# Head 0's k and v into early rows, a priority for weight pieces, and 2600 more projection columns ahead of the first scan

## The chip, the cores and the metric

The kernel runs on one core of a Trainium2 chip. TensorE (PE) multiplies, VectorE (DVE) and ScalarE (ACT) work element by element, GpSimd (POOL) does a few of the same, and SyncE (SP) issues nearly all DMA transfers. The metric is the device time of one execution in microseconds (us), as the median over several runs; lower is better.

## The reference

One layer of a hybrid backbone. 512 latent and 256 context tokens of width 2048 are normalised and modulated, and go through one input projection. Group A is a gated delta rule with 8 heads; group B is attention with 8 query and 2 key heads. Both are gated, concatenated and go through one output projection. What matters here is group A:

```python
qkv = jax.nn.silu(centred_conv(qkv, conv_w))          # 5 taps along the tokens
q, k, v = split(qkv)                                  # per head, 128 wide
q = l2_norm(q) * (HEAD_DIM ** -0.5)
k = l2_norm(k)
g = -jnp.exp(a_log) * jax.nn.softplus(gates + dt_bias)
...
g_c = jnp.cumsum(g)                                   # inside a chunk of 64 tokens
t_inv = triangular_solve(eye + a, eye)                # a: 64 x 64, from k, beta and g_c
u = t_inv @ (v_c * b_c)
w = t_inv @ (k_beta * jnp.exp(g_c))
s_final, o = lax.scan(step, s0, (q_c, k_c, u, w, g_c, intra))
```

The scan runs over 12 chunks, once in each direction.

## The kernel before

Matrices are multiplied in full 32-bit precision as three matmuls of a reduced format: each operand is split into a high and a low half (`whi`, `wlo`). A weight piece is 512 rows by 128 columns: SP loads it (`wraw`), ACT casts the high half (L129), DVE subtracts for the low half (L130). Each of the three has three buffers in turn, so piece i can be cast only when PE has left piece i - 3.

**The stages.** Up to about 157 us the modulation is computed while k, v and q of head 0 and k and q of head 1 are projected into five PSUM banks (`klat`, `vlat`, `qlat`, `cctx` for the context part). The first weights are read by ACT and POOL. The second stage, up to about 240 us, prepares head 0 (`gdn_prep(0)`) while PE projects other columns. Then come eight scans (`gdn_scan`), each beside the preparation of the next head, then attention and the output projection.

**Second stage.** `take` (L195) copies a projected bank to SBUF: into one of three rows `craw`, whose memory only becomes free when the first stage's pool `p0` closes, or into one of two rows `xraw`, which have a pool of their own. Then `gdn_post_k`, `_q` and `_v` run the convolution: ACT starts it (`cacc`, one buffer), DVE adds four taps for latent and context tokens (L221), ACT takes a tanh (L224, L225), DVE makes the SiLU (L237) and writes `kq`, `kc` or `vv`. The gates run beside it: `gates(0, 1)` for head 0 and `gates(1, 8)` for the rest give log decays `gg` on DVE, PE sums them along the chunk (`gcp`, `gtot`, L547 to L551), ACT takes exponentials (L553 to L558), and PE transposes the sums (`gtr`).

**`gdn_prep`.** PE transposes k and q (`t1`, `t2`, `t3`, L640 to L653), ACT copies them and takes sums of squares (L643, L649, L657), PE makes the products `gq` (L693) and `gc` (L709). DVE forms the triangular matrix (`gr`) and transposes blocks of it (`NT`, L718). SP sends them through DRAM (`nd`) into another layout (`NE`), DVE inverts 16 x 16 blocks there in 14 steps (L738, L740), and SP brings them back through DRAM (`DD`, L758). DVE transposes (`DT`, L763), and three rounds on PE (`pxa`, `pxb`, `pxy`) join the blocks to the inverse `UU`, which the scan's first matmul reads (`tsh`, L875). `t1`, `t3` and `gc` share one PSUM bank, `t2` and `gq` another.

**What sets the order.** PE's order is as written (`manual_schedule`): a generator `feed` gives the projection matmul by matmul, and `pull(n)` takes n columns of it between two steps of the preparation or the scan. On ACT, DVE, POOL and SP a scheduler orders the instructions when the program is built, by priorities and by times that it estimates; `tc.high_priority(offset=...)` moves what stands under it ahead. On the chip each engine runs its list in order. Tiles of the projection are named by their target: `kvl`, `kvx` are keys and values of the attention (latent, context), `q0a` the queries of its head 0, `vl`, `kl`, `ql` v, k and q of the delta rule.

Of the kernel before, what the change touches and what calls it, by code (L numbers as in the profile page):

```python
# [8 lines left out]
F32 = mybir.dt.float32  # L9
# [59 lines left out]
def build(tc, a):  # L69
    nc = tc.nc  # L70
    V, S, G, T, SY = nc.vector, nc.scalar, nc.gpsimd, nc.tensor, nc.sync
# [31 lines left out]
    def hpass(k, hi, lo):  # L103

        return (hi, [t[:, k] for t in hh]), (hi, [hl(m, k) for m in range(2)]), (lo, [t[:, k] for t in hh])
# [20 lines left out]
    def split(raw, nm, lo_eng=None):  # L126
        hi = wp.tile([128, 512], F32R, tag="whi", bufs=3, name=f"whi_{nm}")
        lo = wp.tile([128, 512], F32R, tag="wlo", bufs=3, name=f"wlo_{nm}")
        S.copy(hi, raw)  # L129
        (lo_eng or G).tensor_tensor(out=lo, in0=raw, in1=hi, op=ALU.subtract)  # L130
        return hi, lo

    def wpiece(src, nm, shape, lo_eng=None):
        raw = wp.tile([128, 512], F32, tag="wraw", bufs=3, name=f"wraw_{nm}")
        v = raw
        if shape is not None:
            v = raw.rearrange("p (a b) -> p a b", b=shape)
        SY.dma_start(v, src)
        hi, lo = split(raw, nm, lo_eng)
        if shape is not None:  # L140
            hi = hi.rearrange("p (a b) -> p a b", b=shape)
            lo = lo.rearrange("p (a b) -> p a b", b=shape)
        return hi, lo

    def mm3(out, lh, ll, rh, rl, start, stop):
        T.matmul(out, lhsT=lh, rhs=rh, start=start, stop=False, skip_group_check=True)  # L146
        T.matmul(out, lhsT=lh, rhs=rl, start=False, stop=False, skip_group_check=True)  # L147
        T.matmul(out, lhsT=ll, rhs=rh, start=False, stop=stop, skip_group_check=True)  # L148

    def proj_tile(col, nm, pl, pc=None):  # L150
        for _ in proj_steps(col, nm, pl, pc):
            pass

    def proj_steps(col, nm, pl, pc=None):


        for kq in range(4):
            src = w_in[kq * 512:(kq + 1) * 512, col:col + 128].rearrange("(k p) c -> p k c", p=128)
            hi, lo = wpiece(src, f"{nm}_{kq}", 128, V)
            passes = [(kq * 4 + k4, n, lw, rt) for k4 in range(4)  # L160
                      for n, (lw, rt) in enumerate(hpass(kq * 4 + k4, hi[:, k4], lo[:, k4]))]

            def one(out, m, k, n, lw, rt):
                T.matmul(out, lhsT=lw, rhs=rt[m], start=k == 0 and n == 0, stop=k == KT - 1 and n == 2,  # L164
                         skip_group_check=True)

            if pc is not None and kq == 0:
                for out, m, n_ in ((pl, 0, SEQ), (pc, 1, CTX)):
                    for x in passes:
                        one(out, m, *x)  # L170
                        yield n_
                continue
            for x in passes:
                one(pl, 0, *x)
                if pc is not None:
                    one(pc, 1, *x)
                yield SEQ if pc is None else SEQ + CTX
# [11 lines left out]
    def btile(shape, nm):  # L189
        return PB.tile(shape, F32, tag="b", name=nm)  # L190

    def stile(shape, nm, tag):
        return PQ.tile(shape, F32, tag=tag, name=nm)

    def take(pl, pc, raw=None, eng=None):  # L195

        raw = next_craw() if raw is None else raw
        copy = S.copy if eng is None else eng.tensor_copy
        if pc is not None:
            copy(raw[:, 2:2 + CTX], pc)  # L200
        copy(raw[:, CTX + 4:CTX + 4 + SEQ], pl)
        return raw

    def conv(t, nm, raw, ctx):

        n = SEQ + (CTX + 2 if ctx else 0)
        off = n - SEQ
        if not ctx:
            raw = raw[:, CTX + 2:]
        acc = cvp.tile([128, 770], F32, tag="cacc", bufs=CA_BUFS, name=f"cacc_{nm}")  # L210
        acc = acc[:, :n]

        def w(j):
            return cvT[:, j * 24 + t:j * 24 + t + 1]

        e = raw[:, 2:]
        S.activation(acc, raw[:, 0:n], AF.Copy, scale=w(0))
        for i0, m in ((off, SEQ), (0, CTX))[:2 if ctx else 1]:
            for j in range(1, 5):
                x = acc[:, i0:i0 + m]  # L220
                V.scalar_tensor_tensor(out=x, in0=raw[:, i0 + j:i0 + j + m], scalar=w(j), in1=x,  # L221
                                       op0=ALU.mult, op1=ALU.add)
        if ctx:
            S.activation(e[:, :CTX], acc[:, :CTX], AF.Tanh)  # L224
        S.activation(e[:, off:off + SEQ], acc[:, off:], AF.Tanh)  # L225
        return acc, e, off
# [27 lines left out]
    es_x = ExitStack()  # L254
    px_ = es_x.enter_context(tc.tile_pool(name="px", bufs=1, side="right", reuse_waits="tile"))
    xraw = [px_.tile([128, 774], F32, name=f"xraw{i}") for i in range(2)]
# [229 lines left out]
    klat = PP.tile([128, SEQ], F32, tag="pl", name="klat0")  # L486
    vlat = PP.tile([128, SEQ], F32, tag="pl", name="vlat0")
    qlat = stile([128, SEQ], "qlat0", "o")
    klat1 = stile([128, SEQ], "klat1", "k")
    qlat1 = stile([128, SEQ], "qlat1", "s")  # L490
    cctx = PC.tile([128, 2, CTX], F32, tag="pc", name="cctx0")
    cctx1 = btile([128, 2, CTX], "cctx1")
# [74 lines left out]

    es_c = ExitStack()
    cvp = es_c.enter_context(tc.tile_pool(name="cvp", bufs=1, reuse_waits="tile"))
    craw = [cvp.tile([128, 774], F32, name=f"craw{i}") for i in range(3)]  # L570
    for t in craw + xraw:
        for i in (0, CTX + 2, NTOK + 4):
            G.memset(t[:, i:i + 2], 0.0)
    ncraw = [0]

    def next_craw():

        ncraw[0] += 1
        return craw[ncraw[0] % 3]

    qkp = es_g.enter_context(tc.tile_pool(name="qkp", bufs=1, reuse_waits="tile"))
    o_d = dram.tile([8, 128, SEQ], F32, name="o_d")
# [5 lines left out]
    def kq_of(h):  # L588
        if h not in kqs:
            kqs[h] = qkp.tile([128, 8, 128], F32, tag="kq", bufs=3, name=f"kq{h}")  # L590
        return kqs[h]
# [12 lines left out]
    def gdn_post_q(h, raw):  # L604
        kq = kq_of(h)
        acc, e, off = conv(h, f"q{h}", raw, False)
        x, y = [t[:, :SEQ].rearrange("p (c t) -> p c t", t=64) for t in (acc, e)]
        silu(V, kq[:, 0:4, 64:128], x[:, 0:4], y[:, 0:4])
        silu(V, kq[:, 4:8, 0:64], x[:, 4:8], y[:, 4:8])

    def gdn_post_v(h, raw):
        vv = vvs[h] = qkp.tile([128, 6, 2, 64], F32, tag="vv", bufs=1, name=f"vv{h}")
        acc, e, off = conv(16 + h, f"v{h}", raw, True)
        for p0_, n, o in ((2, 4, off), (0, 2, 0)):
            x, y = [t[:, o:o + n * 128].rearrange("p (c t) -> p c t", t=64) for t in (acc, e)]
            silu(V, vv[:, p0_:p0_ + n, 0], x[:, 0:n], y[:, 0:n])
            silu(V, vv[:, p0_:p0_ + n, 1], x[:, n:2 * n][:, ::-1], y[:, n:2 * n][:, ::-1])
# [415 lines left out]
        return tc.high_priority(offset=2500)  # L1033

    with tc.high_priority(offset=4000):
        raws = [take(klat, cctx[:, 0]), take(qlat, None), take(vlat, cctx[:, 1], None, V),
                take(klat1, cctx1[:, 0], xraw[0]), take(qlat1, None, xraw[1])]
    gdn_post_k(0, raws[0])
    gdn_post_q(0, raws[1])
    gdn_post_v(0, raws[2])  # L1040
    gp = es_g.enter_context(tc.tile_pool(name="gp", bufs=1, reuse_waits="tile"))
    ktoks = [gp.tile([128, 6, 2, 128], F32, name=f"ktok{i}") for i in range(2)]
    for i in range(2):
# [54 lines left out]
    def feeding():  # L1098

        yield from feed_kva(0)  # L1100
        yield from feed_qa(0)
        yield from feed_kva(1)
        yield from feed_v(1)
        for h in range(2, NH):
            yield from feed_k(h)
            yield from feed_q(h)
            yield from feed_v(h)
            if h in (3, 5):
                yield from feed_qa(1) if h == 3 else feed_kva(2)
        yield from feed_kva(3)  # L1110
        fed.add("kva")
        for h in range(2, NH):
            yield from feed_qa(h)
        for h in range(NZA):
            yield from feed_za(h)

    feed = feeding()
    debt = [0]

    def pull(n):  # L1120
        debt[0] += n
        while debt[0] > 0:
            c = next(feed, None)
            if c is None:
                debt[0] = 0
                return
            debt[0] -= c

    def run(gen, *pulls):

        for n in pulls:
            pull(n)
            if next(gen, gen) is gen:
                return
        for _ in gen:
            pull(2000)
# [19 lines left out]
    with first_of_all():  # L1156
        next(g1)
    gdn_post_q(1, raws[4])
    es_x.close()
    pull(7000)  # L1160
    next(prep, None)
    run(g1, 7000)
# [2 lines left out]
    UUs.append(gp2.tile([128, 12, 128], F32, name="UU1"))  # L1165
    zero(UUs[1].rearrange("p a d -> p (a d)"))
    run(prep, 5000, 24000, 5000, 7000, 6000)
    tail = None
    for h in range(NH):
        while (h + 1 if h + 1 < NH else "kva") not in fed:  # L1170
# [365 lines left out]
    for c in range(4):  # L1536
# [9 lines left out]
        for k in range(KT):  # L1546
            hi = op_.tile([128, 512], F32R, name=f"wlh{k}")
            lo = op_.tile([128, 512], F32R, name=f"wll{k}")
# [5 lines left out]
        for t in range(4):  # L1554
            ts_ = slice(t * 128, t * 128 + 128)
            f = fr[:, t:t + 1]
# [7 lines left out]
            else:  # L1564
                fl = op_.tile([128, 2], F32, name="fl")
                for q in range(2):
# [3 lines left out]
                    for k in range(KT):  # L1570
                        hi, lo = [w[:, hs] for w in wlast[k]]
# [47 lines left out]
```

## Time and profile before

| What | Value |
|---|---|
| Median of 3 runs (lowest to highest) | 1296.88 us (1294.81 to 1297.11) |
| The profiled execution | 1292.93 us, of which its span is 1291.1 us |
| PE busy, share of the span | 1241.8 us, 96% |
| DVE busy | 849.4 us, 66% |
| ACT busy | 580.7 us, 45% |
| Mean granted TensorE clock | 0.991 |
| 160 to 180 us: busy PE, DVE, ACT; clock | 19.74, 15.40, 13.35 us; 0.85 |
| 180 to 200 us: busy PE, DVE, ACT; clock | 17.86, 19.70, 11.51 us; 1.00 |

The trace's times start at the first instruction of the span. A row of the timeline gives start, length, engine, line, operation, the tile that is written and those that are read; in brackets stands how long the engine was idle before it and which instruction released it. Rows of neighbouring instructions overlap a little. A wait for several engines is put down to the one that came last. "issue" is a time in which the engine waited for nothing that the profile shows.

### The profile page before, as it was taken

Reading aid. Unit: us, or ns where it says so; the run is one execution under the profiler, and the core shown is the slowest. Engines: PE = TensorE matmul, PEld = TensorE weight load, DVE = VectorE, ACT = ScalarE, POOL = GpSimd, SP = SyncE. Lnnn points to the kernel's source line nnn. Section 1 sums busy time; section 2 is a strip of 40 time slices with the busy share of each in tenths; the row PEclk is TensorE's granted clock in tenths of the full one; section 3 lists DMA queues with packets and bytes.
Section 4 is the critical chain, followed back from the end, with each engine's and each line's share of the span. In section 5 each row is a group of like instructions: output and inputs, shape, how many; then the busy total and the mean of one; then the engine's idle time right before and its main releaser. Section 6 shows DMA issues by size and latency. Waiting matters only on the chain. (4 is left out here: it accounts for less than half of the span.)

```text
span 1291.1 us, 24373 instructions
## 1 busy us (share of the span) xinstructions
PE 1241.8 (96%) x9242; PEld 1015.1 (79%) x9242; DVE 849.4 (66%) x1905; ACT 580.7 (45%) x1452; POOL 142.7 (11%) x206
## 2 busy tenths in 40 slices
PE   6899999999999999999999999999999999999997
PEld 4566688878788888888888787777888888788886
DVE  5444586686876769676786646546998997555333
ACT  5222363444545454454644444444455544434211
POOL 1323100111111111111211111100000000000000
PEclk9899999999999999999999999999999999999999
DMA  9999424232222312322232445347445353576302
GB/s 355 319 334 346 134 67 106 55 75 56 67 68 75 72 51 71 76 62 65 62 72 63 104 93 150 102 132 255 136 139 156 109 144 97 174 236 195 90 33 98
DMA packets 227288, 164.53 MB, mean 127 GB/s; under 512 B 62242, under 2 KB 198523, under 8 KB 226147
## 3 DMA queue, kind: packets, MB, share of 16 engines
q1 hardware_dynamic: 226874, 162.87, 43.5%
q8 instruction: 73, 1.20, 0.4%
q14 instruction: 44, 0.36, 0.1%
q10 hardware_dynamic: 297, 0.11, 0.0%
HBM read 148.85 MB, written 14.08 MB: 126 GB/s over the span
## 5 line engine op out<-in xcount | busy, mean ns | idle before, releaser
L240 POOL TENSOR_TENSOR sdh<-sth,egl 128x256 f32<-128x256 f32 x80 | 56.8, 711 | 447.9 <-DVE sth L892 345.3
L871 ACT ACTIVATE oqh<-ksh,egsw 64x128 f32<-64x128 f32 x128 | 46.4, 362 | 93.2 <-DVE rh L866 86.9
L866 DVE SCALAR_TENSOR_TENSOR rh<-ksh,negeg,vtokh 64x128 f32<-64x128 f32 x176 | 61.2, 348 | 31.0 <-PE ksh L854 24.4
L146 PE MATMUL po<-whi_wo,mh 128*128 128x512 f32 x192 | 76.2, 397 | 0.0
L148 PE MATMUL po<-whi_wo,ml 128*128 128x512 f32 x192 | 76.0, 396 | 0.0
L147 PE MATMUL po<-wlo_wo,mh 128*128 128x512 f32 x192 | 76.0, 396 | 0.0
L1358 PE MATMUL zl<-hhL,whi_z 128*128 128x512 f32 x176 | 71.4, 405 | 0.0
L1358 PE MATMUL zl<-hL,whi_z 128*128 128x512 f32 x176 | 69.8, 397 | 0.0
L1358 PE MATMUL zl<-hhL,wlo_z 128*128 128x512 f32 x176 | 69.3, 394 | 0.0
L130 DVE TENSOR_TENSOR wlo_wo<-wraw_wo,whi_wo 128x512 fp32r<-128x512 f32 x48 | 33.1, 690 | 51.5 <-ACT whi_wo L129 51.3
L886 PE MATMUL tsh<-vsh,ktok 128*128 128x128 f32 x352 | 56.6, 283 | 6.9 <-ACT vnh L882 3.5
L886 PEld LDWEIGHTS tsh<-vsh,ktok 128*128 128x128 f32 x352 | 47.3, 190 | 16.2 <-ACT vnh L882 8.1
L129 ACT CAST whi_wo<-wraw_wo 128x512 fp32r<-128x512 f32 x48 | 29.7, 620 | 62.3 <-PE po L148 52.1
L892 DVE TENSOR_TENSOR sth<-sdh,tsh 128x256 f32<-128x256 f32 x80 | 33.6, 420 | 27.4 <-PE tsh L886 19.2
L879 ACT ACTIVATE vsh<-tsh,cch 128x128 f32<-128x128 f32 x88 | 32.2, 366 | 38.8 <-PE tsh L875 37.5
L950 ACT CAST pth<-pt 128x512 fp32r<-128x512 f32 x48 | 26.5, 586 | 44.3 <-PE pt L1287 44.3
L164 PE MATMUL vl<-hhL,whi_v 128*128 128x512 f32 x112 | 46.3, 413 | 0.0
L164 PE MATMUL vl<-hhL,wlo_v 128*128 128x512 f32 x112 | 46.2, 413 | 0.0
L164 PE MATMUL vl<-hL,whi_v 128*128 128x512 f32 x112 | 45.8, 409 | 0.0
L1406 DVE SCALAR_TENSOR_TENSOR gacc<-graw,scol,gacc 128x512 f32<-128x512 f32 x60 | 44.9, 748 | 1.1
L146 PEld LDWEIGHTS po<-whi_wo,mh 128*128 128x128 f32 x192 | 36.1, 188 | 9.5 <-ACT ze L1312 0.8
L148 PEld LDWEIGHTS po<-whi_wo,ml 128*128 128x128 f32 x192 | 36.2, 188 | 8.8
(545 smaller groups left out, 3894.5 us busy)
## 6 DMA issues: line engine op xcount, KB each, us to landing
wada<-in_w_ada SPq DMA_DIRECT2D x64, 512.0 KB, 8.4
graw<-in_w_ada SPq DMA_DIRECT2D x64, 256.0 KB, 3.2
wraw_wo<-in_w_out SPq DMA_DIRECT2D x48, 256.0 KB, 3.1
wraw_z<-in_w_in SPq DMA_DIRECT2D x44, 256.0 KB, 3.0
wraw_v<-in_w_in SPq DMA_DIRECT2D x28, 256.0 KB, 2.9
wraw_k<-in_w_in SPq DMA_DIRECT2D x24, 256.0 KB, 2.8
wraw_q<-in_w_in SPq DMA_DIRECT2D x24, 256.0 KB, 2.8
xs<-in_x SPq DMA_DIRECT2D x4, 1024.0 KB, 5.2
```

The lines of the kernel that those rows point to most:

```text
L130: (lo_eng or G).tensor_tensor(out=lo, in0=raw, in1=hi, op=ALU.subtract)
L146: T.matmul(out, lhsT=lh, rhs=rh, start=start, stop=False, skip_group_check=True)
L147: T.matmul(out, lhsT=lh, rhs=rl, start=False, stop=False, skip_group_check=True)
L148: T.matmul(out, lhsT=ll, rhs=rh, start=False, stop=stop, skip_group_check=True)
L164: T.matmul(out, lhsT=lw, rhs=rt[m], start=k == 0 and n == 0, stop=k == KT - 1 and n == 2, skip_group_check=True)
L240: eng.tensor_tensor(out=out, in0=x, in1=y, op=ALU.mult)
L866: V.scalar_tensor_tensor(out=r[rows], in0=ks[rows, d], scalar=gsc["negeg"][rows, gcol:gcol + 1], in1=vtok[rows, p], op0=ALU.mult, op1=ALU.add)
L871: S.activation(oq[rows, v, p - 2], ks[rows, d], AF.Copy, scale=gsc["egsw"][rows, gcol:gcol + 1])
L886: T.matmul(ts[:, d], lhsT=ktok[:, p, half], rhs=vs, start=True, stop=True, skip_group_check=True)
L892: V.tensor_tensor(out=sn, in0=sd, in1=ts[:, 0:2], op=ALU.add)
L1358: T.matmul(pl, lhsT=lw, rhs=rt, start=k == 0 and m == 0, stop=k == KT - 1 and m == 2, skip_group_check=True)
L1406: V.scalar_tensor_tensor(out=acc, in0=raw, scalar=scol[:, k:k + 1], in1=acc, op0=ALU.mult, op1=ALU.add)
```

## The change

Three edits in the second stage. First, head 0's k goes into `xraw[0]` and its v into `xraw[1]`; q of head 0 and k and q of head 1, two of which had those rows, go into `craw`. There are four `craw` rows now, and the pool of `xraw` closes earlier. Second, every weight piece that `proj_steps` loads and splits is given a priority of 2000 (`urgent`) from the start of `feed` until just before the first scan, and 0 after it. Third, `pull(2600)` takes 2600 more columns of projection after the last step of `gdn_prep(0)`, before the scan of head 0.

```diff
--- before.py
+++ after.py
@@ -147,6 +147,8 @@
         T.matmul(out, lhsT=lh, rhs=rl, start=False, stop=False, skip_group_check=True)
         T.matmul(out, lhsT=ll, rhs=rh, start=False, stop=stop, skip_group_check=True)
 
+    urgent = [0]
+
     def proj_tile(col, nm, pl, pc=None):
         for _ in proj_steps(col, nm, pl, pc):
             pass
@@ -156,7 +158,8 @@
 
         for kq in range(4):
             src = w_in[kq * 512:(kq + 1) * 512, col:col + 128].rearrange("(k p) c -> p k c", p=128)
-            hi, lo = wpiece(src, f"{nm}_{kq}", 128, V)
+            with tc.high_priority(offset=urgent[0]):
+                hi, lo = wpiece(src, f"{nm}_{kq}", 128, V)
             passes = [(kq * 4 + k4, n, lw, rt) for k4 in range(4)
                       for n, (lw, rt) in enumerate(hpass(kq * 4 + k4, hi[:, k4], lo[:, k4]))]
 
@@ -567,7 +570,7 @@
 
     es_c = ExitStack()
     cvp = es_c.enter_context(tc.tile_pool(name="cvp", bufs=1, reuse_waits="tile"))
-    craw = [cvp.tile([128, 774], F32, name=f"craw{i}") for i in range(3)]
+    craw = [cvp.tile([128, 774], F32, name=f"craw{i}") for i in range(4)]
     for t in craw + xraw:
         for i in (0, CTX + 2, NTOK + 4):
             G.memset(t[:, i:i + 2], 0.0)
@@ -576,7 +579,7 @@
     def next_craw():
 
         ncraw[0] += 1
-        return craw[ncraw[0] % 3]
+        return craw[ncraw[0] % 4]
 
     qkp = es_g.enter_context(tc.tile_pool(name="qkp", bufs=1, reuse_waits="tile"))
     o_d = dram.tile([8, 128, SEQ], F32, name="o_d")
@@ -1033,11 +1036,12 @@
         return tc.high_priority(offset=2500)
 
     with tc.high_priority(offset=4000):
-        raws = [take(klat, cctx[:, 0]), take(qlat, None), take(vlat, cctx[:, 1], None, V),
-                take(klat1, cctx1[:, 0], xraw[0]), take(qlat1, None, xraw[1])]
+        raws = [take(klat, cctx[:, 0], xraw[0]), take(vlat, cctx[:, 1], xraw[1], V), take(qlat, None),
+                take(klat1, cctx1[:, 0]), take(qlat1, None)]
     gdn_post_k(0, raws[0])
-    gdn_post_q(0, raws[1])
-    gdn_post_v(0, raws[2])
+    gdn_post_q(0, raws[2])
+    gdn_post_v(0, raws[1])
+    es_x.close()
     gp = es_g.enter_context(tc.tile_pool(name="gp", bufs=1, reuse_waits="tile"))
     ktoks = [gp.tile([128, 6, 2, 128], F32, name=f"ktok{i}") for i in range(2)]
     for i in range(2):
@@ -1114,6 +1118,7 @@
         for h in range(NZA):
             yield from feed_za(h)
 
+    urgent[0] = 2000
     feed = feeding()
     debt = [0]
 
@@ -1156,7 +1161,6 @@
     with first_of_all():
         next(g1)
     gdn_post_q(1, raws[4])
-    es_x.close()
     pull(7000)
     next(prep, None)
     run(g1, 7000)
@@ -1165,6 +1169,8 @@
     UUs.append(gp2.tile([128, 12, 128], F32, name="UU1"))
     zero(UUs[1].rearrange("p a d -> p (a d)"))
     run(prep, 5000, 24000, 5000, 7000, 6000)
+    pull(2600)
+    urgent[0] = 0
     tail = None
     for h in range(NH):
         while (h + 1 if h + 1 < NH else "kva") not in fed:
```

PE's order is the same up to the first scan. In three places the order on other engines is this.

ACT at the end of the first projection. `klat_492`, `qlat_494` and `cctx_497` are head 0's, `klat_495`, `qlat_496` and `cctx_498` head 1's; `whi_kv_2` is the third piece of the first attention key projection. Before:

```order
L201 COPY xraw_121<-klat_495 128x512
L200 COPY xraw_121<-cctx_498 128x256
L129 CAST whi_kv_2_1725<-wraw_kv_2_1723 128x512
L201 COPY xraw_122<-qlat_496 128x512
L462 ACTIVATE beta<-gx 128x96
L200 COPY craw_1553<-cctx_497 128x256
L201 COPY craw_1553<-klat_492 128x512
L201 COPY craw_1554<-qlat_494 128x512
L217 ACTIVATE cacc_k_1585<-craw_1553,cvT 128x770
L467 ACTIVATE ug<-ug 128x96
```

With the change:

```order
L204 COPY xraw_121<-klat_492 128x512
L203 COPY xraw_121<-cctx_497 128x256
L129 CAST whi_kv_2_1730<-wraw_kv_2_1728 128x512
L465 ACTIVATE beta<-gx 128x96
L204 COPY craw_1553<-qlat_494 128x512
L203 COPY craw_1554<-cctx_498 128x256
L204 COPY craw_1554<-klat_495 128x512
L204 COPY craw_1555<-qlat_496 128x512
L470 ACTIVATE ug<-ug 128x96
L220 ACTIVATE cacc_k_1589<-xraw_121,cvT 128x770
L129 CAST whi_kv_3_1780<-wraw_kv_3_1778 128x512
```

The copies of `klat_492` and its context now stand ahead of the cast of `whi_kv_2`, the others behind it, and the cast of `whi_kv_3` has moved up behind the start of conv k.

ACT between conv k and the first transposes of head 0. `egl` to `egsw` are the exponentials of the gate sums, `cacc_q` is conv q of head 0. Before:

```order
L129 CAST whi_kv_3_1775<-wraw_kv_3_1773 128x512
L229 ACTIVATE UU_2180<-cmain 128x1536
L217 ACTIVATE cacc_q_1601<-craw_1554,cvT 128x512
L129 CAST whi_q0a_1835<-wraw_q0a_1833 128x512
L558 ACTIVATE egl<-gtot_1744 128x12
L553 ACTIVATE negeg<-gcp_1743 128x12
L554 ACTIVATE esuf<-gcp_1743 128x12
L556 ACTIVATE egsw<-gcp_1743 64x12 x2
L558 ACTIVATE egl<-gcp_1743 128x12
L129 CAST whi_q0a_1879<-wraw_q0a_1877 128x512
L225 ACTIVATE craw_1554<-cacc_q_1601 128x512
```

With the change:

```order
L228 ACTIVATE xraw_121<-cacc_k_1589 128x512
L232 ACTIVATE UU_2184<-cmain 128x1536
L227 ACTIVATE xraw_121<-cacc_k_1589 128x256
L561 ACTIVATE egl<-gtot_1749 128x12
L556 ACTIVATE negeg<-gcp_1748 128x12
L557 ACTIVATE esuf<-gcp_1748 128x12
L559 ACTIVATE egsw<-gcp_1748 64x12 x2
L561 ACTIVATE egl<-gcp_1748 128x12
L220 ACTIVATE cacc_q_1605<-craw_1553,cvT 128x512
L129 CAST whi_q0a_1884<-wraw_q0a_1882 128x512
L228 ACTIVATE craw_1553<-cacc_q_1605 128x512
```

The start of conv q stood ahead of the exponentials and stands behind them now; the casts of `whi_kv_3` and the first `whi_q0a` have left for places further up.

DVE in the preparation of head 0. `grh` is the triangular matrix, `cch` the scale columns, `cacc_k` conv k of head 1, `wlo_kv_0` the low half of the first piece of the second attention key projection. Before:

```order
L240 TENSOR_TENSOR cch_1865<-cch_1865,esuf 128x12
L240 TENSOR_TENSOR IB_1638<-gqh_1886,grh_1785 64x4x64 x4
L221 SCALAR_TENSOR_TENSOR cacc_k_2000<-xraw_121,cvT,cacc_k_2000 128x512
L702 TENSOR_TENSOR grh_1785<-grh_1785,cch_1865 128x768
L221 SCALAR_TENSOR_TENSOR cacc_k_2000<-xraw_121,cvT,cacc_k_2000 128x512
L240 TENSOR_TENSOR grh_1785<-gqh_1886,grh_1785 128x256 x2
L240 TENSOR_TENSOR grh_1785<-gch_1942,grh_1785 128x128 x2
L718 STREAM_TRANSPOSE NTh_1789<-grh_1785 32x6x32 x4
L221 SCALAR_TENSOR_TENSOR cacc_k_2000<-xraw_121,cvT,cacc_k_2000 128x512
L221 SCALAR_TENSOR_TENSOR cacc_k_2000<-xraw_121,cvT,cacc_k_2000 128x256
L130 TENSOR_TENSOR wlo_kv_0_2028<-wraw_kv_0_2025,whi_kv_0_2027 128x512
```

With the change:

```order
L243 TENSOR_TENSOR IB_1643<-gqh_1891,grh_1790 64x4x64
L680 TENSOR_SCALAR cch_1870<-cch_1870 128x12
L243 TENSOR_TENSOR cch_1870<-cch_1870,esuf 128x12
L224 SCALAR_TENSOR_TENSOR cacc_k_2005<-craw_1554,cvT,cacc_k_2005 128x512
L130 TENSOR_TENSOR wlo_kv_0_2033<-wraw_kv_0_2030,whi_kv_0_2032 128x512
L705 TENSOR_TENSOR grh_1790<-grh_1790,cch_1870 128x768
L224 SCALAR_TENSOR_TENSOR cacc_k_2005<-craw_1554,cvT,cacc_k_2005 128x512
L243 TENSOR_TENSOR grh_1790<-gqh_1891,grh_1790 128x256
L130 TENSOR_TENSOR wlo_kv_1_2079<-wraw_kv_1_2076,whi_kv_1_2078 128x512
L243 TENSOR_TENSOR grh_1790<-gqh_1891,grh_1790 128x256
L224 SCALAR_TENSOR_TENSOR cacc_k_2005<-craw_1554,cvT,cacc_k_2005 128x512
```

The low half stood behind the block transposes and five steps of conv k, and now stands behind the first of these steps. A low half of the next piece has come in as well.

## The prediction

> **What bounds the kernel now.** First the page's busy shares, then the waits of TensorE (PE) between 140 and 345 us, where the change sits, then that stretch in order of time on PE, ScalarE (ACT) and VectorE (DVE).
>
> ```profile
> PE 1241.8 (96%) x9242; PEld 1015.1 (79%) x9242; DVE 849.4 (66%) x1905; ACT 580.7 (45%) x1452; POOL 142.7 (11%) x206
> ```
>
> PE is the bound: 49.3 us of the 1291.1 us span are not matmul. The edit adds no matmul and removes none, so it can only move PE's idle time and the clock it is granted. In the stretch that it touches, PE waits for this (engine, tile, line, releaser; total us, times, longest):
>
> ```profile
> PE kvl L164 <- DVE wlo_kv L130: 2.1, 1, 2.1
> PE kvl L164 <- DVE craw L201: 2.1, 1, 2.1
> ...
> PE tsh L875 <- DVE UU L821: 0.9, 1, 0.9
> ...
> PE t1h L640 <- DVE kq L237: 0.3, 1, 0.3
> ```
>
> Each part of the edit answers one of the first three rows. The fourth, 0.3 us, is small but tells the most: PE already arrives no later than its data there. The same waits on PE's timeline (start us, length, instruction, and in brackets the idle time before it):
>
> ```profile
> 157.40 0.39 PE L422 MATMUL qlat<-hhL,wlo_w 128*128 128x512 f32 x1
> 159.85 0.77 PE L164 MATMUL kvl<-hhL,whi_kv 128*128 128x512 f32 x1 [2.06 <-DVE craw L201]
> 160.42 0.63 PE L164 MATMUL kvl<-hL,whi_kv 128*128 128x512 f32 x1
> 160.84 0.63 PE L164 MATMUL kvl<-hhL,wlo_kv 128*128 128x512 f32 x1
> ...
> 171.03 0.28 PE L164 MATMUL kvx<-hhC,wlo_kv 128*128 128x256 f32 x1
> 171.15 0.39 PE L164 MATMUL kvl<-hhL,whi_kv 128*128 128x512 f32 x1
> 171.38 0.28 PE L164 MATMUL kvx<-hhC,whi_kv 128*128 128x256 f32 x1
> ...
> 173.59 0.95 PE L547 MATMUL gcp<-gg__116,ctri 128*128 128x6 f32 x8
> ...
> 178.24 0.66 PE L640 MATMUL t1h<-cmain,kq 128*128 128x128 f32 x4 [0.26 <-DVE kq L237]
> ...
> 186.14 1.09 PE L693 MATMUL gqh<-kq 128*64 128x128 f32 x16
> ...
> 198.32 0.51 PE L164 MATMUL kvl<-hhL,wlo_kv 128*128 128x512 f32 x1 [2.14 <-DVE wlo_kv L130]
> ```
>
> The first gap costs more than its 2.06 us, as the granted clock shows (stretch, its length, busy time of five engines, then PEclk):
>
> ```profile
> 160.00:165.00 5.00, 5.00 (x12) 3.94 (x13) 4.28 (x16) 5.00 (x7) 0.00 (x0) 0.50 0.20 52
> 167.00:172.00 5.00, 5.00 (x30) 4.38 (x30) 3.45 (x15) 3.24 (x4) 0.00 (x0) 1.00 0.23 56
> 199.00:204.00 5.00, 5.00 (x32) 4.41 (x31) 5.00 (x15) 1.77 (x3) 0.00 (x0) 1.00 0.74 176
> ```
>
> After it PE runs at half clock: matmuls of 512 columns come 0.42 us apart (160.42 to 160.84) until 165.98, against 0.23 (171.15 to 171.38; 256 columns 0.12) later. From 159.85 that is 6.13 us at half speed, 3.07 us lost on top. After the 2.14 us gap at 196 the clock stayed at 1.00. A gap of two microseconds may or may not cost the clock.
>
> **Early rows: the first gap goes.** Why is the bank of klat late?
>
> ```profile
> 157.64 0.62 ACT L129 CAST whi_kv<-wraw_kv 128x512 fp32r<-128x512 f32 x1 [2.20 <-issue]
> ...
> 159.08 0.60 ACT L201 COPY craw<-klat 128x512 f32<-128x512 f32 x1
> ...
> 161.05 2.87 ACT L229 ACTIVATE ktok<-cmain 128x1536 f32<-128x1536 f32 x2
> 163.79 2.01 ACT L229 ACTIVATE IB<-cmain 128x1024 f32<-128x1024 f32 x2
> 165.68 0.64 ACT L225 ACTIVATE craw<-cacc_k 128x512 f32<-128x512 f32 x1
> ```
>
> The copy that empties klat of head 0 stands on ACT behind a cast that waits until PE is done with its last weights (157.64) and ends at 159.68; the matmul starts at 159.85. The page names DVE's copy of vlat, which ends in the same instant; both move, so either reading serves. With xraw as target the klat copy stands ahead of that cast. PE then goes straight on at 157.64: -2.06, and -3.07 for the clock. Full speed takes 13.74 - 3.07 = 10.67 us to gcp, so PE gets there at 168.3 instead of 173.59.
>
> **Where that gain goes.** Its data are not there. In the new ACT order two weight casts stand ahead of the tanh of conv k, and the first waits until PE has left piece kv_0: 12 matmuls at 0.23 and 12 at 0.12 after 157.64, 161.9. Two casts at 0.55, two zeroings of ktok at 1.4 and two of IB at 1.0 later, tanh starts at about 167.8 against 165.68. The first rows of kq follow, and behind them on DVE the gate logs gg, 0.3 us later than now:
>
> ```profile
> 168.98 0.16 DVE L540 SCALAR_TENSOR_TENSOR gg__116<-zg,ag 128x12 f32<-128x12 f32 x1
> ...
> 174.99 0.74 DVE L221 SCALAR_TENSOR_TENSOR cacc_q<-craw,cvT,cacc_q 128x512 f32<-128x512 f32 x1
> 175.65 0.17 DVE L559 TENSOR_SCALAR negeg<-negeg 128x12 f32<-128x12 f32 x1
> ...
> 177.77 0.75 DVE L237 SCALAR_TENSOR_TENSOR kq<-craw,cacc_q 128x256 f32<-128x256 f32 x2
> 178.44 1.36 DVE L536 SCALAR_TENSOR_TENSOR ug<-ug,w_g 128x84 f32<-128x84 f32 x5
> ...
> 197.58 0.68 DVE L130 TENSOR_TENSOR wlo_kv<-wraw_kv,whi_kv 128x512 fp32r<-128x512 f32 x1
> ```
>
> gg ends at about 169.4, PE takes gcp at 169.5: a new wait of 1.2 us. Worse, conv q now stands on ACT behind the exponentials that wait for gcp (it stood ahead of them), so all four of its DVE steps come after gcp. gcp and its sums take 1.3 us, to 170.8. Then DVE does, in its new order: gcum, negeg and gts 0.4; two halves of kc 0.4; ten gate steps of heads 1 to 7, three in a row at 0.27 (1.36 / 5), the others about 0.15 each between wider work, 1.9; four conv steps at 0.66 (174.99 to 175.65), 2.6; one low half 0.6; the first half of kq 0.4. That is 6.3 us, with 0.3 for hand-overs 177.4, and t1h can start at 177.5. PE reaches it 4.39 us (178.24 - 0.26 - 173.59) after gcp, at 173.9, and waits 3.6 us. The wait of 0.3 has become the bound: t1h gains 0.7 us, not 5.4.
>
> From there to gqh ACT is the bound. Conv v reuses the one conv buffer, so it starts after kq, at 177.9. The rows for its length and for what now stands between it and gqh:
>
> ```profile
> 179.72 4.32 DVE L221 SCALAR_TENSOR_TENSOR cacc_v<-craw,cvT,cacc_v 128x512 f32<-128x512 f32 x8
> ...
> 180.32 0.28 ACT L643 ACTIVATE NTh<-t1h 128x128 f32<-128x128 f32 x1
> ...
> 180.72 0.28 ACT L643 ACTIVATE NTh<-t1h 128x128 f32<-128x128 f32 x1
> ...
> 189.33 0.62 ACT L129 CAST whi_kv<-wraw_kv 128x512 fp32r<-128x512 f32 x1 [0.31 <-PE qal0a L164]
> ```
>
> ACT's start of conv v 0.9, DVE's eight steps 4.3: 183.1. Its two tanh 0.9: 184.0. All four squares of t2 (0.40 each, 180.32 to 180.72) now stand behind them, with two copies of kv, one of t3 and a cast among them (0.3 + 0.5 + 0.35 + 0.55): 187.3. gqh reuses the bank of t2 and waits for the last square: 187.3 instead of 186.14, 1.1 us later, if the clock stays up. If the 3.6 us wait costs the clock (after 2.06 us it did), PE loses 1.7 to 3.3 us on the way and arrives at 187.1 to 188.7. I take 187.7: at gqh the change is 1.6 us **behind** (-2.06 - 3.07 + 1.2 + 3.3 = -0.6 at t1h, then +2.2).
>
> The skill has a rule on this. The Trainium skill, "TensorE: Matmul & The Clock Gate", Part 1, says PE drops to half clock after at least one idle window of about 3.4 us and returns after one busy window. Taken strictly, the present 2.06 us gap would not drop the clock and my -3.07 would be missing, while the new 3.6 us wait may drop it: the sum below would be +1.7 instead of -1.4. The row at 160 to 165 shows the drop after 2.06 us, so I keep the measurement; the rule speaks against the change.
>
> **Priority for the pieces: the second gap goes.** wlo_kv of the second kv projection runs at 197.58 though its high half was cast at 189.33 to 189.95; conv k and the solve's steps stood ahead. In the new order it comes right after the scale columns cch, on my times 191.5 to 192.1, and PE wants it at 196.18 + 1.6 = 197.8. So -2.14, and the change is 0.5 us ahead. The cover is 5 us.
>
> **2600 more columns ahead of the first scan.** These are five matmuls of 512, 1.2 us that are done anyway; UU's last copies run meanwhile: -0.9. Later ones are not created: the projection ends with the same pieces left. Copies into a fourth craw cost nothing: no row above waits for a craw but the first. The sum is 1.6 - 2.14 - 0.9 = **-1.4 us**.
>
> What the trace cannot give is the scans. Five matmuls further on, other weight pieces and convs stand beside each step, and PE's waits of 235 to 880 us are dealt anew:
>
> ```profile
> L886 PE MATMUL tsh<-vsh,ktok 128*128 128x128 f32 x352 | 56.6, 283 | 6.9 <-ACT vnh L882 3.5 <-ACT vsh L879 3.1
> ...
> L875 PE MATMUL tsh<-rh,UU 128*128 128x128 f32 x176 | 37.0, 292 | 4.4 <-DVE rh L866 3.8
> ...
> L857 PE MATMUL ksh<-sth,kc 128*128 128x256 f32 x48 | 14.8, 390 | 1.5 <-DVE sth L890 1.2 <-DVE sth L892 0.2
> ...
> L875 PE MATMUL tsh<-vtokh,UU 128*128 128x128 f32 x16 | 3.4, 294 | 2.2 <-DVE UU L821 2.2
> ```
>
> 15 us in all, none above 1.2. All could go or as many come; a fifth, 3 us either way, is my bound, and I take nothing. The profiled execution took 1292.93 us (span 1291.1 and 1.8 around it); -1.4 gives 1291.5. The runs' median stands 3.95 us above it, so I predict 1295.4 on the scale of the runs.
>
> **Rivals.** *The first gain stays* (faster): my hand-made queue after gcp is too long, t1h waits under 1.5 us and gqh not at all. For it: DVE was busy only 3.45 of the 5 us from 167 to 172, and a shorter wait keeps the clock. Against: the order is fixed, and the 6.3 us hold no idle time. All terms: -2.06 - 3.07 - 0.26 - 2.14 - 0.9 = -8.4, 1288.5; half of the t1h delay kept, -6, 1290.9.
>
> *The solve's chain becomes the bound* (slower):
>
> ```profile
> 222.60 0.57 DVE L763 STREAM_TRANSPOSE DTh<-DDh 128x384 f32<-128x384 f32 x1
> ...
> 226.95 0.22 PE L771 MATMUL pxah<-DTh,grh 32*32 32x32 f32 x2
> ```
>
> DT is ready 3.8 us before PE takes it. The same priority puts weight transfers on SP ahead of the solve's own (v_1 amid ndh, v_2 ahead of NEh, k_1 ahead of DDh), each waiting for a low half on DVE, and wlo_k_0 ahead of this transpose. I have the chain 2 us late at NT and 3 at the transpose: 0.8 short of deciding. From 3.8 us on each further microsecond is PE's, and a long one costs the clock; 6 us late: +2.2 + 3.07 - 1.4 = +3.9, 1300.8.
>
> *It doesn't do what it says*: the gap at 157.6 has another owner, say the kv pieces, and stays with its clock; t1h is then late as before, and the second gap and UU are given back in the scans: 0, 1296.9.
>
> **How the numbers follow.** Forecast 0.48, with 1292.5 to 1298 (clock 1.6 and scans 3, not both at their ends); first gain stays 0.24; solve's chain 0.16; nothing 0.12. About 0.2%, 2.6 us, is what a measurement can tell: faster is under 1294.3. A quarter of the forecast, nearly all of the first rival: 0.35. Slower, over 1299.5: most of the solve rival and a little of the forecast, 0.15. The same 0.50. The range 1289.5 to 1300 takes in the clock, the scans and most of both rivals.
>
> **What would show it.** Right: no gap at kvl and clock 1.00 from 158 to 168; a wait of about 1 us at gcp and 3 to 4 us at t1h, with half clock after it or a wait at gqh, PE at gqh near 187.7; no wait for wlo_kv near 196; no UU wait at the first scan. Wrong: t1h before 176, a wait at pxah, or scan waits that change by more than 3 us.

## The result and the profile after

| | Before | With the change |
|---|---|---|
| Median of the runs (lowest to highest) | 1295.0 us (1294.0 to 1297.1) | 1306.9 us (1304.5 to 1312.0) |
| Ratio, 95% interval | | 1.0092 (1.0069 to 1.0111) |
| The profiled execution, its span | 1292.9 us, 1291.1 us | 1307.7 us, 1305.9 us |
| PE busy | 1241.8 us | 1248.4 us |
| Mean granted TensorE clock | 0.991 | 0.985 |

The change makes the kernel 11.9 us slower; the prediction said 1295.4 us, 1289.5 to 1300. Where on the way the time is lost, the first matmul of some tiles on PE's timeline shows. In the table stands when PE reaches it before, and how much later it does with the change (the first stage came out 0.4 us later in this execution: its last matmul starts at 157.80 instead of 157.40):

| First | Before, us | With the change |
|---|---|---|
| kvl (second stage) | 159.85 | -1.8 |
| t1h | 178.24 | +1.4 |
| gqh | 186.14 | +4.3 |
| pxah | 226.95 | +2.2 |
| tsh of the first scan | 239.73 | +2.6 |
| tsh of the third scan | 393.77 | +3.7 |
| tsh of the fourth scan | 472.24 | +10.5 |
| tsh of the fifth scan | 547.68 | +13.4 |
| s, the first of the attention | 877.96 | +14.9 |

At the first scan 1.2 us of the 2.6 are the five matmuls that are done earlier. So the second stage costs about 1 us, and the scans some 12. **The second stage** on PE's timeline of the changed kernel (columns as in the prediction):

```profile
158.03 0.40 PE L167 MATMUL kvl<-hhL,whi_kv 128*128 128x512 f32 x1
...
169.99 1.03 PE L550 MATMUL gcp<-gg__116,ctri 128*128 128x6 f32 x8 [0.91 <-DVE gg__116 L543]
...
179.66 1.12 PE L643 MATMUL t1h<-cmain,kq 128*128 128x128 f32 x4 [3.64 <-DVE kq L240]
...
190.47 1.09 PE L696 MATMUL gqh<-kq 128*64 128x128 f32 x16 [0.42 <-ACT NTh L652]
```

The gap at kvl is gone, 0.91 us of wait at gcp and 3.64 at t1h have come. The granted clock in this stretch (stretch, its length, busy time of five engines, PEclk):

```profile
171.00:174.00 3.00, 3.00 (x14) 2.50 (x14) 1.45 (x8) 1.56 (x7) 0.00 (x0) 0.55 0.00 0
...
180.00:183.00 3.00, 3.00 (x12) 2.62 (x11) 2.09 (x5) 2.77 (x10) 0.00 (x0) 0.50 0.00 0
183.00:186.00 3.00, 3.00 (x15) 2.66 (x14) 2.96 (x8) 0.34 (x1) 0.00 (x0) 0.67 0.00 0
```

Half clock follows both waits. Behind t1h it lasts until PE reaches t2h near 185 and costs some 2.5 us. Behind gcp it makes t1h's data later: DVE's conv q stands behind the copy of gtr, and PE reaches that transpose only after the projection columns between, at 173.98. DVE's rows:

```profile
174.43 0.28 DVE L567 COPY gts__117<-gtr 12x128 f32<-12x128 f32 x1 [1.54 <-PE gtr L565]
174.64 0.73 DVE L224 SCALAR_TENSOR_TENSOR cacc_q<-craw,cvT,cacc_q 128x512 f32<-128x512 f32 x1
```

In e2 below, where the clock stayed at 1.00 there, DVE waited 0.20 us instead of 1.54 and t1h came 8.3 us after gcp instead of 9.7. **The scans:** PE's waits from 235 to 890 us of the changed kernel (engine, tile, line, releaser; total, times, longest). `rh` and `sth` are DVE's own short steps of the scan, `vsh` and `vnh` ACT's; all stand between one matmul of the scan and the next:

```profile
PE tsh L878 <- DVE rh L869: 5.5, 11, 1.1
PE tsh L889 <- ACT vsh L882: 5.3, 6, 1.6
PE ql L167 <- DVE wlo_q L130: 3.9, 1, 3.9
PE tsh L889 <- ACT vnh L885: 2.9, 6, 1.6
PE ksh L860 <- DVE sth L893: 2.9, 1, 2.9
PE tsh L878 <- DVE UU L824: 0.8, 2, 0.5
```

And of the kernel before, the same view:

```profile
PE tsh L875 <- DVE rh L866: 3.8, 7, 0.9
PE tsh L886 <- ACT vnh L882: 3.5, 6, 1.1
PE tsh L886 <- ACT vsh L879: 3.1, 5, 0.8
PE tsh L875 <- DVE UU L821: 2.2, 4, 0.9
PE ksh L857 <- DVE sth L890: 1.2, 1, 1.2
```

The third row of the changed kernel is new: a single wait for the low half of a weight piece, in the third scan. PE's timeline there:

```profile
423.70 0.39 PE L167 MATMUL ql<-hL,whi_q 128*128 128x512 f32 x1
428.03 0.80 PE L167 MATMUL ql<-hhL,wlo_q 128*128 128x512 f32 x1 [3.94 <-DVE wlo_q L130]
...
429.48 0.63 PE L167 MATMUL ql<-hL,whi_q 128*128 128x512 f32 x1
429.91 0.63 PE L167 MATMUL ql<-hhL,wlo_q 128*128 128x512 f32 x1
```

After the 3.94 us PE runs at half clock from 428.03 to about 434 (matmuls of 512 columns 0.43 us apart, as at 429.48, instead of 0.23): 3.0 us more, 6.9 together. All listed waits between the first tsh and the first s add up to 22.3 us, and to 14.2 before; this half clock and another after the 2.9 us for sth (clock 0.73 and 0.70 from 798 to 804, some 1.7 us) are most of the rest of the 12 us. Why is the low half late? DVE's rows of the changed kernel:

```profile
417.44 0.76 DVE L243 TENSOR_TENSOR grh<-gqh,grh 128x256 f32<-128x256 f32 x2
418.12 2.86 DVE L224 SCALAR_TENSOR_TENSOR cacc_k<-craw,cvT,cacc_k 128x512 f32<-128x512 f32 x5
...
425.69 1.57 DVE L721 STREAM_TRANSPOSE NTh<-grh 32x192 f32<-32x192 f32 x4
427.29 1.29 DVE L130 TENSOR_TENSOR wlo_q<-wraw_q,whi_q 128x512 fp32r<-128x512 f32 x2
```

and of the kernel before:

```profile
413.70 0.76 DVE L240 TENSOR_TENSOR grh<-gqh,grh 128x256 f32<-128x256 f32 x2
414.37 0.68 DVE L130 TENSOR_TENSOR wlo_q<-wraw_q,whi_q 128x512 fp32r<-128x512 f32 x1
414.97 0.48 DVE L240 TENSOR_TENSOR grh<-gch,grh 128x128 f32<-128x128 f32 x2
415.48 0.77 DVE L718 STREAM_TRANSPOSE NTh<-grh 32x192 f32<-32x192 f32 x2
416.19 0.70 DVE L221 SCALAR_TENSOR_TENSOR cacc_k<-craw,cvT,cacc_k 128x512 f32<-128x512 f32 x1
```

PE's first matmul with this low half, in the kernel before:

```profile
421.47 0.40 PE L164 MATMUL ql<-hhL,wlo_q 128*128 128x512 f32 x1
```

Before, the low half was ready at 415.05, 6.4 us ahead of that matmul; it stood right behind the first half of grh and ahead of conv k of head 4. With the change it stands behind that whole convolution, its SiLU and the block transposes, 9 us of DVE work, though its high half was cast at 415.59 to 416.2.

### The profile page after: what moved, and what is told of

It reads as the page before. It is cut to its first block, busy times and chain, and to the rows that moved or that the text cites. A ratio compares the mean times of both kernels' runs of the same rounds, so it can differ in the third digit from the quotient of the medians.

```text
span 1305.9 us, 24369 instructions
## 1 busy us (share of the span) xinstructions
PE 1248.4 (96%) x9242; PEld 1020.7 (78%) x9242; DVE 852.3 (65%) x1905; ACT 581.5 (45%) x1452; POOL 143.8 (11%) x209
## 5 line engine op out<-in xcount | busy, mean ns | idle before, releaser
L167 PE MATMUL ql<-hhL,wlo_q 128*128 128x512 f32 x96 | 40.2, 419 | 3.9 <-DVE wlo_q L130 3.9
```

## The experiments

Theory A: the third edit, 2600 columns ahead of the first scan, shifts the projection against the scans, so that the planner (the scheduler that orders the other engines when the program is built) places the instructions of DVE and ACT anew in all of them; the loss is in single badly placed pieces. Rival B: the time is lost in the second stage by the early rows, and the scans only pass it on. Each edit was run alone or left out. The ratio is to the kernel before on the same chip, with its 95% interval; the last column is that ratio's distance from 1 times the time before, about 1294 us.

| Run | Early rows | Priority | Columns | Besides | Ratio (interval) | us |
|---|---|---|---|---|---|---|
| the change, and again (e10) | yes | yes | 2600 | | 1.0092 (1.0069 to 1.0111), 1.0094 (1.0077 to 1.0111) | +11.9, +12.2 |
| e1 | | | 2600 | | 1.0086 (1.0070 to 1.0101) | +11.1 |
| e2 | yes | yes | | | 1.0028 (1.0017 to 1.0039) | +3.6 |
| e3 | yes | yes | 2600 | one piece first | 1.0063 (1.0048 to 1.0078) | +8.1 |
| e4 | yes | yes | 2600 | priority kept in the scans | 1.0045 (1.0028 to 1.0062) | +5.8 |
| e5 | | yes | | | 0.9986 (0.9976 to 0.9996) | -1.8 |
| e6 | yes | | | | 1.0034 (1.0022 to 1.0047) | +4.4 |
| e7 | yes | yes | | own buffer for conv q | 1.0012 (1.0004 to 1.0021) | +1.6 |
| e8 | | | 1300 | | 1.0028 (1.0017 to 1.0040) | +3.6 |
| e9 | yes | yes | | buffer, gate logs first | 0.9964 (0.9950 to 0.9978) | -4.7 |
| e11 | yes | yes | 2600 | e4 and e9 together | 0.9987 (0.9977 to 0.9998) | -1.7 |

**e1, the columns alone.**

```diff
     run(prep, 5000, 24000, 5000, 7000, 6000)
+    pull(2600)
```

> The kernel before with the third edit alone: 2600 more columns ahead of the first scan, no early rows, no priority. On DVE, ACT and SP the order from the second scan on is that of the changed kernel. Theory A (the five matmuls pull the projection out of step with the scans, and the schedule that comes of it puts low halves of weights behind a convolution): slower than before by 9 to 13 us, 1304 to 1308 us, with PE waiting about 4 us for wlo_q in the third scan and half clock after it, and the first scan's wait for UU gone. Theory B (the time is lost by the early rows and the late t1h in the second stage, and the scans only pass it on): 0.9 us faster than before to no change, 1294 to 1296 us, no wait over 1.5 us in the scans.

11.1 us slower, and the waits of the changed kernel are all there, in a kernel whose second stage is the one of before:

```profile
PE tsh L886 <- ACT vsh L879: 5.4, 6, 1.6
PE tsh L875 <- DVE rh L866: 5.3, 10, 1.1
PE ql L164 <- DVE wlo_q L130: 3.9, 1, 3.9
```

The wait of 0.9 us for UU at the first scan is gone, as meant. Theory A holds and rival B falls.

**e2, the other two edits without the columns.**

```diff
     run(prep, 5000, 24000, 5000, 7000, 6000)
-    pull(2600)
     urgent[0] = 0
```

> The changed kernel without its third edit: early rows and the priority, no extra columns. On DVE, ACT and SP the order of the scans is that of the kernel before. Theory A: 0.5 to 3 us slower than before (what stood at the first tsh of head 0, +2.6 us, less 1.2 us for the five matmuls, plus 0.9 us for the wait for UU that comes back), 1295.5 to 1298 us; no wait for wlo_q in the third scan. Theory B: 9 to 12 us slower, 1304 to 1307 us.

3.6 us, a little above theory A's bounds and far from B's. In the scans PE waits as it did before, the longest waits 1.4 and 1.0 us, with no low half among them. From the first scan to the seventh the distance to the kernel before stays between 1.3 and 1.8 us.

**e3, one piece placed ahead.** The changed kernel, with the late piece alone given a priority:

```diff
-            with tc.high_priority(offset=urgent[0]):
+            with tc.high_priority(offset=1000 if (nm, kq) == ("q4", 2) else urgent[0]):
```

> The changed kernel, with a priority of 1000 for one weight piece in the scans: the third piece of q of head 4, the one whose low half PE waits 3.9 us for at 428 us. Theory A: that wait goes and the half clock after it too, 3.9 + 3.0 = 6.9 us, so 1299 to 1302 us; the other waits (vnh, vsh, sth of the later scans) stay. Rival C (the wait comes from the convolution on DVE and ACT being late as such, and whatever is put first, the next one is late): the wait moves to the next low half or to the scan's rh, and under 2 us are won, 1305 to 1307 us.

Its low half ran at 418.74, ahead of the convolution, and PE no longer waits for it. What is left of wlo_q in the list is a wait for the next piece, the fourth:

```profile
430.33 0.49 PE L167 MATMUL ql<-hhL,wlo_q 128*128 128x512 f32 x1 [0.43 <-DVE wlo_q L130]
```

From the first scan to the fourth the kernel loses 1.9 us against the kernel before, where the changed one loses 7.9: 6.0 us from one instruction's place in a queue. The spans say 1305.9 against 1299.3, 6.6 us less, the ratios about 4 us with an overlap of intervals. So the mechanism is shown in its place; how much of the 6.9 us stays at the end is less sure. Rival C, that the next piece is late instead, is right only in kind: the next low half is late by 0.43 us where the third was by 3.94, the clock stays at 1.00 after it, and 6.0 us are won up to the fourth scan.

**e4, the priority kept in the scans.**

```diff
-    urgent[0] = 0
+    urgent[0] = 300
     tail = None
```

> The changed kernel, with a priority of 300 for all weight pieces in the scans instead of 0. Theory A: no wait for any low half in the scans, 7 us and more are won back, 1296 to 1301 us; what is left comes from vnh, vsh, rh and sth, which may wait a little longer behind the pieces. Rival C: the scans' own short steps stand behind the pieces instead, and their waits grow by as much as is won: 1304 to 1308 us.

5.8 us slower by the ratio, 1298.4 us, within theory A; some 6 us are won back, a little under its 7. No wait for a low half is left. The scan's own steps still wait longer than before:

```profile
PE tsh L878 <- DVE rh L869: 6.3, 12, 1.1
PE tsh L889 <- ACT vsh L882: 5.5, 6, 1.4
```

With the change alone vsh and rh waited 10.8 us, with the columns alone (e1) 10.7, here 11.8, before 6.9. So they come with the columns; whether the priority adds to them is not clear (the changed kernel taken again, e10, has 11.3). How the columns lengthen them was not tested. One instance, on ACT in the changed kernel, with PE waiting 1.56 us for the vsh in the last row:

```profile
490.43 0.61 ACT L129 CAST whi_q<-wraw_q 128x512 fp32r<-128x512 f32 x1
490.94 0.37 ACT L203 COPY craw<-kx 128x256 f32<-128x256 f32 x1
491.33 0.58 ACT L650 COPY ktok<-t2h 64x512 f32<-64x512 f32 x1
491.94 0.37 ACT L882 ACTIVATE vsh<-tsh,cch 128x128 f32<-128x128 f32 x1
```

**e8, half the columns.**

```diff
     run(prep, 5000, 24000, 5000, 7000, 6000)
+    pull(1300)
```

> The kernel before with three extra matmuls (1300 columns) ahead of the first scan instead of five. On DVE the third piece of q of head 4 stands ahead of the convolution there, as in the kernel before. Theory A (what costs is where the schedule puts single pieces, and each shift deals that anew): no wait for wlo_q and no half clock in the third scan, waits of the other kinds up to 5 us more than before: 0 to 6 us slower, ratio 1.000 to 1.005. Rival D (taking columns ahead of the first scan costs as such, because the later scans lack them as cover): about three fifths of what 2600 columns cost, 6 to 7 us slower, ratio 1.0045 to 1.0055, spread over all the scans.

3.6 us slower. The piece that was late with 2600 columns is not, and up to the start of the fourth scan nothing is lost: PE is 0.7 us ahead of the kernel before there. In the fourth scan 4.3 us go. On DVE a low half stands behind another convolution:

```profile
483.83 3.27 DVE L221 SCALAR_TENSOR_TENSOR cacc_k<-craw,cvT,cacc_k 128x512 f32<-128x512 f32 x6
...
491.01 0.69 DVE L130 TENSOR_TENSOR wlo_q<-wraw_q,whi_q 128x512 fp32r<-128x512 f32 x1
```

and on PE:

```profile
491.75 0.50 PE L164 MATMUL ql<-hhL,wlo_q 128*128 128x512 f32 x1 [2.81 <-DVE wlo_q L130]
```

Half clock after it (0.74 and 0.69 from 491 to 497) costs 1.7 us more. Theory A's ratio came in. Its sentence that no wlo_q would wait in the third scan held, but in the fourth another one did, 2.8 us. Rival D, a loss spread over all scans, falls.

**e5 and e6, the priority and the early rows alone.**

```diff
...
+    urgent[0] = 2000
     feed = feeding()
...
```

> The kernel before with the second edit alone: the priority for weight pieces until the first scan. The prediction's step: the gap of 2.14 us before wlo_kv near 196 us goes and nothing else changes, so about 2.1 us faster, ratio 0.998 to 0.999; gaps at kvl (2.1 us) and half clock after it as before. Rival (the solve's chain of DMA transfers and transposes is pushed back by the pieces and PE waits at pxah, or the gain is given back as a longer wait for UU): no change, ratio 0.9995 to 1.001.

1.8 us faster where 2.1 were expected. The wait for wlo_kv is gone from the second stage's list; at pxah PE now waits 0.7 us, so the chain of the solve stands close behind. From gqh to pxah PE takes 39.4 us instead of 40.8: the 2.14 us less those 0.7.

```diff
-        raws = [take(klat, cctx[:, 0]), take(qlat, None), take(vlat, cctx[:, 1], None, V), ...
+        raws = [take(klat, cctx[:, 0], xraw[0]), take(vlat, cctx[:, 1], xraw[1], V), take(qlat, None), ...
...
```

> The kernel before with the first edit alone: early rows, four craw. The prediction's step says 1.6 us behind at gqh, ratio 1.001. From the trace of the changed kernel without its third edit (3.6 us behind at gqh, of which the half clock after t1h is 2.8 and not 1.6) I now expect 3 to 4 us behind at gqh and the gap at wlo_kv still there: 3 to 5 us slower, ratio 1.002 to 1.004. Rival (it is the priority that makes t1h late): under 1.5 us slower, ratio under 1.0012.

4.4 us slower: taken alone, the early rows cost and the priority wins. The rows pay two waits:

```profile
PE t1h L640 <- DVE kq L237: 3.9, 1, 3.9
PE kvl L164 <- DVE wlo_kv L130: 3.2, 1, 3.2
```

The gap that was 2.14 us before has grown to 3.2. The priority takes it away in the kernel with both edits.

The ratio came in, but not the place. PE comes to gqh at 186.10, level with before (186.14) and not 3 to 4 us behind. It waits for nothing at gcp, and half clock behind t1h costs 1.6 us. It is 1.6 us behind from pxah to the first scan and 3.0 at the first matmul of the attention. So the wait at gcp belongs to the priority: ACT starts the tanh of conv k at 165.63 here, and at 168.04 with the change, where two weight casts (162.34 and 166.57) stand ahead of it.

**e7, a buffer of its own for conv q of head 0.**

```diff
-        acc = cvp.tile([128, 770], F32, tag="cacc", bufs=CA_BUFS, name=f"cacc_{nm}")
+        acc = cvp.tile([128, 770], F32, tag="cacq" if nm == "q0" else "cacc", bufs=CA_BUFS, name=f"cacc_{nm}")
```

> Early rows and priority without the third edit, and conv q of head 0 gets a buffer of its own, so that it need not wait until conv k has left the one buffer and stands ahead of the gates' exponentials again. The order of the scans stays that of the kernel before. Theory (t1h is late because conv q stands behind the sums of the gates, and its wait of 3.9 us costs 2.8 us of clock): the wait at t1h falls under 1 us, no half clock, and against the same kernel without the buffer 3.9 + 2.8 = 6.7 us at most come back at t1h, some of it lost again at gqh, where ACT was 0.4 us late: 3 to 6 us faster than that kernel, 1 to 3 us faster than the kernel before, ratio 0.998 to 0.9995. Rival (DVE has no room: 15 to 16 of 20 us are busy there, and moving conv q forward pushes gg back, so that gcp waits as much longer): no change against that kernel, ratio 1.002 to 1.004.

ACT starts conv q at 163.44 instead of 172.62, t1h comes at 177.15 instead of 178.63, and gqh at 185.05 instead of 189.69: 4.6 us won there, of which 1.5 at t1h and most of the rest from a clock that stays up. At pxah only 0.9 us of it are left:

```profile
PE gcp L550 <- DVE gg__116 L543: 3.5, 2, 2.1
PE t1h L643 <- DVE kq L240: 1.3, 1, 1.3
```

One of the two gcp waits is new, 2.1 us near 204: the gate logs of heads 1 to 7 (203.44 on DVE, 178.83 without the buffer) had moved behind the block transposes of head 0 (194.26), and half clock followed that wait as well. Neither the theory's range nor the rival's came in: 2.0 us won by the ratios against the kernel without the buffer, and still 1.6 slower than before.

**e9, the gate logs ahead too.**

```diff
     pull(9000)
-    next(g1)
+    with tc.high_priority(offset=200):
+        next(g1)
```

> The kernel with early rows, priority and a buffer of its own for conv q (no third edit), and besides a priority of 200 for the gate logs of heads 1 to 7, which had fallen behind the block transposes there and let PE wait 2.1 us at the second gcp, with 1.5 us or so of half clock after it. Theory (each wait in this stage is a place in DVE's queue): that wait and the clock go, 3 to 4 us less than without it: 1290 to 1292 us where the kernel before takes 1293.5, ratio 0.9965 to 0.999. Rival (DVE is too full, and the gate logs push the steps of gdn_prep back, so that PE waits at pxah or for wlo_kv instead): no gain, ratio 1.000 to 1.002.

1289.9 us, 4.7 us faster than before and the fastest of all, a little beyond the theory's range; the wait near 204 is gone and the clock is 1.00 from 140 to 240 us. The rival's wait at pxah is there too, 0.9 us, but does not take the gain. So early rows can stand in a faster kernel: without columns, with a place for conv q and for the gate logs. Whether those two would win as much without the early rows was not run.

```profile
PE gcp L550 <- DVE gg__116 L543: 1.3, 1, 1.3
PE t1h L643 <- DVE kq L240: 1.3, 1, 1.3
PE pxah L774 <- DVE DTh L766: 0.9, 1, 0.9
```

**e10 and e11, the changed kernel beside its mended form.** The latter has all three edits with the amendments of e4 and e9.

> The changed kernel as it is, beside the others on one chip: 11 to 13 us slower than before, ratio 1.0085 to 1.010, so that the ratios of the single edits can be set against it. If the edits add up (rows and priority 3.6 us, columns 11 us) it is 14 us, 1.011.

> The changed kernel with all three edits and three amendments: priority of 300 for weight pieces in the scans, a buffer of its own for conv q of head 0, priority of 200 for the gate logs of heads 1 to 7. Theory: the scans' late pieces (7 to 8 us) and the second stage's waits (5 to 6 us) both go, and what is left against the kernel before are the longer waits for vsh, rh and sth in the scans (5 us by the kernel with the priority alone) less what the second stage wins: -1 to +3 us, ratio 0.999 to 1.0025. Rival (the gains are one and the same time, and the scans take up whatever the second stage wins): as the kernel with priority kept alone, ratio 1.004 to 1.006.

12.2 us slower, and 1.7 us faster, just beyond the theory's range: 13.9 us between them, where the repairs won some 6 (e4) and 8 us (e9 against e2) singly. So the two add up, as nearly as the intervals tell. It remains behind e9 by 3 us, with longer waits for rh and vsh in its scans (11.4 us, there 6.7); those for sth are the same. The columns buy nothing here.

## Why the prediction was wrong

**The failed step** is the sentence on the scans: "All could go or as many come; a fifth, 3 us either way, is my bound, and I take nothing." Some 12 us came. The bound was taken from the waits that were there, 15 us in all and none above 1.2, and nothing in the trace stands behind the fifth. The largest piece of what came is of another kind: a low half that was ready 6.4 us before PE wanted it (at 415.05 for 421.47), and so stood in no list of waits, was put behind a convolution. A list of waits shows what is late, not what could be. The same paragraph says rightly that the waits "are dealt anew"; e1 shows that this deal alone is 11 of the 12 us, e3 that one piece is most of what is lost up to the fourth scan. With no low half late (e4) 5.8 us stay, in the second stage and in longer waits for the scan's own steps.

**Early rows** went as worked out in the waits: 0 at kvl, 0.91 at gcp (forecast 1.2), 3.64 at t1h (3.6). The wait at gcp, though, comes with the priority and not with the rows (e6). Mis-sized was the clock. PE came to gqh at 190.5 instead of 187.7. Of these 2.8 us, 0.6 were there when DVE took the sums of gcp (171.4 instead of 170.8; 0.4 of them from the first stage). The next 1.5 are a wait that was not counted: the prediction took the copy of gtr with its 0.3 us of work alone, and behind the half clock after gcp it waited 1.54. The remaining 0.6 lie between t1h and gqh: 10.2 us were forecast, 10.8 came (7.9 before), 0.4 of them a wait at gqh and some 2.5 half clock. So 1.6 us behind at gqh was 4.3, or 3.9 without the first stage. The gain of 3.07 us at kvl was itself the price of one execution: after the same gap half clock cost 1.7 in e5 and e8.

**Priority** was right: -2.14 forecast, -1.8 alone (e5). **The first scan's UU** was right too: its 0.9 us went. **The fourth craw** shows no wait of its own in any of the traces; it was not run alone.

**The rivals.** *The first gain stays* fell, since t1h waited 3.6 us; with conv q in a buffer and the gate logs ahead it nearly holds (e9). *The solve's chain becomes the bound*: PE waits 0.2 us at pxah with the change and 0.7 to 0.9 in e5 and e9, so the chain is late by little here and is the next bound of this stage. *It doesn't do what it says* fell. No rival had the scans as the place of the loss; the list of what would prove it wrong did: "scan waits that change by more than 3 us". They changed by 8.

Open is why the sum of e1 and e2 (14.7 us) is above the whole (11.9 and 12.2); the intervals of each, about 2 us, could make it up. What moves vsh and rh when the columns are added was read in one instance only, not tested. Open too is where the early rows alone lose the rest of their 4.4 us, of which the trace shows 1.6 at the first scan and 3.0 at the attention.

## What to carry to other kernels

Where a planner sets the order of the other engines, an edit that shifts the main engine's work by a microsecond can change their queues in every later stage: compare the two orders there too, and look for pieces with a deadline that have moved behind a long run of work, whatever the list of waits says of them. Give such pieces a lasting priority when anything is shifted; here it took back 6 of the 12 us (e4). A wait that is removed in a full stage is only the first in a row: mend the next ones (e7, e9) before the gain is counted.

## What the runs showed of the hardware

What a gap on PE costs in granted clock does not follow from its length; the same gap may cost it or not. In the kernel with rows alone (e6) PE waited 3.20 us for wlo_kv, until 199.90, and kept its clock (columns as above):

```profile
195.00:198.00 3.00, 1.70 (x7) 1.03 (x6) 2.84 (x8) 1.10 (x2) 0.00 (x0) 1.00 0.21 33
198.00:201.00 3.00, 1.10 (x5) 0.91 (x6) 3.00 (x9) 0.94 (x2) 0.00 (x0) 1.00 0.46 121
```

The wait of 1.33 us at the first gcp left the clock at 1.00 in e9:

```profile
170.00:172.00 2.00, 1.03 (x10) 1.05 (x10) 1.22 (x6) 0.36 (x1) 0.00 (x0) 1.00 0.28 83
```

In e11, which has the same second stage, it dropped after the same wait:

```profile
170.00:172.00 2.00, 1.68 (x13) 1.67 (x14) 0.67 (x6) 0.05 (x1) 0.00 (x0) 0.81 0.00 1
172.00:174.00 2.00, 2.00 (x7) 1.71 (x8) 1.60 (x4) 1.63 (x7) 0.00 (x0) 0.50 0.00 0
```

So too for 0.91 us at gcp in the changed kernel (0.55 from 171 to 174), against 1.00 in e2 after 0.92 us. After the 2.06 us at kvl half clock lasted 6.1 us in the kernel before and 3.4 in e5; after the 3.9 us for wlo_q about 6 us in the changed kernel and 3.4 in e10. Over all runs a gap of 0.9 to 4 us cost between nothing and 3.1 us of clock. The Trainium skill, "TensorE: Matmul & The Clock Gate", Part 1, ties the drop to at least one idle window of about 3.4 us and says that this window runs freely. That the same gap costs once and not another time agrees with a window that runs freely; that the clock dropped after 0.91 and 1.33 us does not agree with a whole idle window.
